# Three pairs of attention-side gate chunks by seven block products

## The chip, the cores and the metric

One core of one Trainium2 chip runs the whole program. The metric is device time in microseconds (us). The engines are TensorE (PE, with its weight loads listed as PEld), VectorE (DVE), ScalarE (ACT), GpSimd (POOL) and SyncE (SP); each works through a queue of its own in order. DMAs are issued from SP's, ACT's and POOL's queues.

## The reference

One decoder block on 512 tokens of 1024 features, in fp32: a feed-forward layer, a token-mixing layer, a second feed-forward layer. What matters here is the mixing layer on its normalised input `u`:

```
z = u @ w_in
gate_br, x_br, q, k, v, g_lru, g_attn = jnp.split(z, IN_SPLITS, axis=-1)
...
y_lru = rg_lru(conv(x_br)) * gelu(gate_br)
y_attn = sliding_window_attention_with_sinks(rope(q), rope(k), v, attn_sinks)
merged = sigmoid(g_lru) * (y_lru @ w_proj_lru) + sigmoid(g_attn) * (y_attn @ w_proj_attn)
return merged @ w_out
```

The change concerns `g_attn = u @ w_in[:, 4608:]`, a product of 512 x 1024 with 1024 x 1024.

## The kernel before

**Split products.** Every fp32 operand is split into a high part (a cast to fp32r) and a low part (the rest). `mm3` (L166 to L169) issues three matmuls for one product: high x high, high x low, low x high. For weights, `wload` starts a DMA on SP's queue into a `wraw` buffer (L105), `wround` casts it on ACT (L115), `wsplit` subtracts on DVE (L123); `wget` returns the next split weight and asks for the two behind it. The order of weights is the list `worder` (L70 to L91).

**Chunks.** Features lie on partitions, tokens along the free dimension. `feat_chunk` (L238) computes 128 output features for all 512 tokens: 8 blocks of 128 inputs, three matmuls of 512 columns each, 24 in all. Normalised features are `u2`, four buffers: high and low parts of two halves, written by `to_features` at the end of the first feed-forward layer.

**The mixing layer** (L1122 to L1214) goes on in this order: `x_group(0)`, keys (`k_pair`), values, `x_group(1)`, two `q_pair`s, eight `gate_chunk`s (`gt`) with attention steps between, two more `q_pair`s, and then eight times `sig_gate` for the LRU side (`glg` the gate chunk, `glp` the projection chunk) and eight times for the attention side (`gag`, `gap`). `k_pair` and `q_pair` rotate on POOL, write to DRAM and load back in another layout (`qt<-q_halves`). `attend(g, n)` handles head group g and token block n; the list `todo` gives their order; its first matmuls are named `at<g><n>b`. `tick` advances work that was begun with `start`.

**The attention side** (L1199 to L1214): `sig_gate(c, ya, "ga")` computes gate chunk c, its tanh on ACT (`gas`), projection chunk c from the split attention output `ya0`, `ya1`; then two DVE instructions (L1201, L1202) multiply and add the LRU side's `m1` into `mg`. POOL starts the DMAs that form sums of blocks of the output weight (`osums`). `oop_split` (L1183) splits what the output projection `token_out` needs (`oy`).

**Seven products.** The feed-forward layers already compute some of their columns by `paired` (L346): the 2 x 2 blocks of two chunks' weights (loaded as `L` and `R`) are summed on DVE (`M`, `N`, L365), split into `W1` to `W4` (L375, L376), and multiplied with sums of blocks of the features that `moving` (L738) makes and splits, and `blocks` takes straight from the features. Seven products of 12 matmuls of 256 columns then give two chunks, accumulated in three PSUM banks X, Y and Q, with copies of X in between (`sn`, `sw`) and adds on DVE.

**Order and buffers.** Where no `manual_schedule` stands, a planner puts the instructions in order before the program runs: among those that its own model of durations counts as ready it takes the earliest in program order. `token_out` and the second feed-forward layer stand in the order written. SBUF buffers of 8 KB per partition (`b8`) come from a pool of 19, those of 4 KB (`t4`) from a pool of 8, those of 2 KB (`t2`) from 10; PSUM has 8 banks. A buffer's next user waits until all users of the previous tile are done.

Of the kernel before, what the change touches and what calls it, by code (L numbers as in the profile page):

```python
# [8 lines left out]
F32 = mybir.dt.float32  # L9
F32R = mybir.dt.float32r  # L10
AF = mybir.ActivationFunctionType
ALU = mybir.AluOpType
# [4 lines left out]
P = 128  # L17
# [6 lines left out]
T = 512  # L24
NT = T // P
# [14 lines left out]

@with_exitstack
def hybrid_block_kernel(ctx, tc, x, xt, g1, w_first, gains, gu1, gs1, dn1, w_x, w_gate, w_q, w_k, w_v, w_gl, w_ga, w_pl, w_pa,
                        w_o, gu2, gs2, dn2, vecs, bd, sinks, rope, mask, out):
    nc = tc.nc
    V, A, G, PE, SP = nc.vector, nc.scalar, nc.gpsimd, nc.tensor, nc.sync

# [17 lines left out]
    def b8(name, shape, dtype=F32):  # L64
        return big.tile(shape, dtype, name=name, tag="b8")
# [9 lines left out]
    for gu, dn in ((gu1, dn1), (gu2, dn2)):  # L75
        worder += [gu[j, i] for j in range(gu.shape[0]) for i in range(2)]
        caps.append(len(worder))
        sums = [dram.tile([P, KS * 512], F32, name=f"wsum{len(wsum)}{i}") for i in range(4)]
        s1, s2, s3, s4 = sums
        wsum[len(wsum)] = (dn, sums)  # L80
        for w in (dn[0], dn[1], s4, s2, s1, s3, dn[3]):
            worder += [w[:, i:min(i + 1024, KS * 512)] for i in range(0, KS * 512, 1024)]
        if gu is gu1:
            worder += [w_x[c] for c in range(4)] + [w_k[i] for i in range(2)] + [w_v[i] for i in range(2)]
            worder += [w_x[c] for c in range(4, 8)] + [w_q[i] for i in range(4)]
            worder += [w_gate[c] for c in range(8)] + [w_q[i] for i in range(4, 8)]
            worder += [w[c] for c in range(8) for w in (w_gl, w_pl)]
            worder += [w[c] for c in range(8) for w in (w_ga, w_pa)]
            t1, t2_, t3, t4_ = osum
            for w in (w_o[0], w_o[1], t2_, t1, w_o[3], t3, t4_):  # L90
                worder += [w[:, i:i + 1024] for i in (0, 1024)]  # L91
# [861 lines left out]
    def x_group(gi):  # L953
        a4, m4, bx4 = (b8(f"{n}{gi}", [P, 4, T]) for n in ("la", "lm", "lb"))
        hl.append(m4)
        cr = range(4 * gi, 4 * gi + 4)
        if gi == 0:
            high_half(u2, x_low, lambda c, b: start(lru_chunk(c, b, a4, m4, bx4, c == cr[-1])),
                      key_weights, 1)
        else:  # L960
            for c in cr:
                w = wget()
                b = bank(f"x{c}")
                feat_chunk(b, w, u2, ALL)
                tick()
                start(lru_chunk(c, b, a4, m4, bx4, c == cr[-1]))
# [139 lines left out]
    def sig_gate(c, src, name):  # L1106
        w = wget()
        b = bank(f"{name}g{c}")
        feat_chunk(b, w, u2, ALL)
        s = t2(f"{name}s{c}")  # L1110
        A.activation(s, b, AF.Tanh, scale=0.5)
        tick()
        wh, wl = wget()
        b = bank(f"{name}p{c}")
        for k in range(KD):
            ks = slice(k * P, (k + 1) * P)
            sh, sl = src[k // 4]
            mm3(b, wh[:, ks], wl[:, ks], sh[:, k % 4, :], sl[:, k % 4, :], k == 0, k == KD - 1)
        tick()
        return s, b  # L1120

    qts = {}  # L1122
    norms = []
    x_group(0)
    kp = [b8(f"kp{i}", [P, 2, 2, T], F32R) for i in range(2)]
    vt = b8("vt", [P, NT, NKV, 2, HD], F32R)
    start(k_pair(kp))
# [2 lines left out]
    for m in range(2):  # L1130
        start(q_pair(m))
    y0 = b8("ya0", [P, 4, T])
    todo = [(g, n) for n in range(NT) for g in range(2)]

    def next_attend(*a):
        if todo:
# [34 lines left out]
    start(split_y(y1, "ya1"))  # L1171
    while live:
        tick()
    mg = [b8(f"mg{i}", [P, 4, T]) for i in range(2)]
    lo_, hi_ = slice(0, 256), slice(256, 512)
    a11, a21, a12, a22 = (mg[i][:, :, tok] for i in range(2) for tok in (lo_, hi_))
    oop = {}
# [18 lines left out]
        V.tensor_tensor(out=o, in0=a, in1=b, op=f)  # L1196
        return o

    for c in range(KD):  # L1199
        s, b = sig_gate(c, ya, "ga")  # L1200
        V.scalar_tensor_tensor(out=s, in0=s, scalar=1.0, in1=b, op0=ALU.add, op1=ALU.mult)  # L1201
        V.tensor_tensor(out=mg[c // 4][:, c % 4, :], in0=s, in1=m1[c // 4][:, c % 4, :], op=ALU.add)  # L1202
        if c < 4:
            o, a, _ = oplan[c]
            with tc.issue_after(norms[-1].ins):
                G.dma_start(osum[o], w_o[a])
        if c in (1, 2, 3, 5):
            o, _, b = oplan[min(c, 4) - 1]
            G.dma_start(osum[o], osum[o // 2] if b is None else w_o[b], accum_op=ALU.add)
        if c == 4:  # L1210
            oop_split(1, a11)
        if c == 5:
            oop_split(7, osum_tile("os3", a11, a21, ALU.subtract))
            oop_split(2, a12, ks=slice(0, 2))  # L1214

    g_post, g_pre = gain_pair(3, 2, "g_b2")
    hs2 = [dram.tile([P, D], F32, name=f"h2_spill{t}") for t in range(NT)]
# [123 lines left out]
def _layout(inputs):  # L1341
    import numpy as np

    c = np.ascontiguousarray
    f = {k: np.asarray(v)[0] for k, v in inputs.items()}
    a = {}
    a["x"] = c(f["x"])
    a["xt"] = c(f["x"].T.reshape(KD, P, T))
    a["g1"] = c(f["ffn1_pre_g"].reshape(KD, P).T)
    a["w_first"] = None  # L1350
    a["gains"] = np.stack([f[n] for n in ("ffn1_pre_g", "ffn1_post_g", "mix_pre_g", "mix_post_g",
                                          "ffn2_pre_g", "ffn2_post_g")])

    def gu(w):
        return c(w.reshape(KD, P, 2, KF, P).transpose(3, 2, 1, 0, 4).reshape(KF, 2, P, D))

    def chunks(w):
        return c(w.reshape(KD, P, KD, P).transpose(2, 1, 0, 3).reshape(KD, P, D))

    a["w_first"] = c(f["ffn1_w_gu"].reshape(KD, P, 2, KF, P)[:, :, :, :2].transpose(0, 1, 3, 2, 4).reshape(KD, P, 512))  # L1360
    def pairs_of(w, j):
        b = w.reshape(2, 4, P, 2, KF // 2, 2, P).transpose(4, 3, 5, 0, 2, 1, 6)[j // 2:].reshape(-1, 2, 2, P, 512)
        return c(np.stack([np.concatenate([b[:, 0, 1], b[:, 0, 0]], 2), np.concatenate([b[:, 1, 0], b[:, 1, 1]], 2)], 1))

    a["gu1"], a["gs1"] = gu(f["ffn1_w_gu"])[2:JSTD["f1"]], pairs_of(f["ffn1_w_gu"], JSTD["f1"])
    ks = [np.concatenate([np.arange(*(GROUPS[g][0], sum(GROUPS[g]))) for g in h]) for h in KHALVES]

    def down_blocks(w):
        w = w.reshape(KF, P, 2, 512)
        return c(np.stack([w[ks[j], :, i].transpose(1, 0, 2).reshape(P, KS * 512) for i in range(2) for j in range(2)]))  # L1370

    a["dn1"] = down_blocks(f["ffn1_w_down"])
    w = f["w_in"]
    a["w_x"], a["w_gate"] = chunks(w[:, D:2 * D]), chunks(w[:, :D])
    half = HD // 2

    def pairs(w):
        return w.reshape(D, -1, 4, 2, half).transpose(0, 1, 3, 2, 4).reshape(D, -1)

    def chunks_of(w):  # L1380
        n = w.shape[1] // P
        return c(w.reshape(KD, P, n, P).transpose(2, 1, 0, 3).reshape(n, P, D))

    a["w_q"], a["w_k"] = chunks_of(pairs(w[:, 2048:3072])), chunks_of(pairs(w[:, 3072:3328]))
    a["w_v"] = c(w[:, 3328:3584].reshape(2, 4, P, 256).transpose(0, 2, 1, 3).reshape(2, P, 1024))
    a["w_gl"], a["w_ga"] = chunks(w[:, 3584:4608]), chunks(w[:, 4608:])
    a["w_pl"] = chunks(f["w_proj_lru"])
    wa = f["w_proj_attn"].reshape(2, 2, 4, HD, D).transpose(0, 2, 1, 3, 4).reshape(D, D)
    a["w_pa"] = chunks(wa)
    w = f["w_out"].reshape(2, 4, P, 2, 512)  # L1390
    a["w_o"] = c(np.stack([w[j, :, :, i].transpose(1, 0, 2).reshape(P, 2048) for i in range(2) for j in range(2)]))
    a["gu2"], a["gs2"] = gu(f["ffn2_w_gu"])[:JSTD["f2"]], pairs_of(f["ffn2_w_gu"], JSTD["f2"])
    a["dn2"] = down_blocks(f["ffn2_w_down"])
    vec = [f["conv_w"][i] for i in range(4)] + [f[n] for n in _VECS]
    a["vecs"] = c(np.stack(vec).reshape(8, KD, P).transpose(2, 0, 1))
    bd = np.zeros((2, 2, HD, KD, 2, HD), np.float32)
    wb = np.stack([f["lru_w_a"], f["lru_w_x"]]).reshape(2, KD, 2, HD, HD)
    for r in range(2):
        bd[:, r, :, :, r, :] = wb[:, :, r].transpose(0, 2, 1, 3)
    a["bd"] = bd.reshape(2, P, D)  # L1400
    a["sinks"] = f["attn_sinks"]
    inv = (10000.0 ** (-np.arange(half) / half)).astype(np.float32)
    ang = np.arange(T, dtype=np.float32)[:, None] * inv[None, :]
    cs = np.stack([np.cos(ang), np.sin(ang)]).astype(np.float32).transpose(2, 0, 1)
    a["rope"] = c(np.tile(cs, (4, 1, 1)))
    qi, si = np.arange(P)[:, None], np.arange(2 * P)[None, :]
    a["mask"] = np.where((si > qi) & (si <= qi + P), 0.0, -1e30).astype(np.float32)
    return a
# [24 lines left out]
```

## Time and profile before

| | |
|---|---|
| median of 3 runs | 1106.77 us (1106.17 to 1107.04) |
| profiled execution | 1106.74 us, of which the span of instructions is 1105.0 us |
| PE busy | 1095.5 us, 6582 matmuls |
| DVE busy | 901.6 us |
| ACT busy | 602.9 us |
| POOL busy | 88.0 us |
| DMA | 213.60 MB, 193 GB/s on average |

A view of lines gives for each instruction its start, its length, the engine, the line of the kernel (that of a helper where one issues it), the operation, the tiles written and read, the shape, and in brackets how long the engine had been idle and what ended that. A group view gives minimum, median and maximum in ns. Rows of DMA issues give the size of one and the median time from issue to landing. The windows view gives a stretch of time: its length, the busy time and number of instructions of PE, PEld, DVE, ACT and POOL, then the granted clock, the share of the DMA engines and GB/s.

### The profile page before, as it was taken

To read this page: it belongs to the slowest core of one execution; us is meant where nothing else is said; L and a number is where in the kernel's file an instruction comes from. 1 tells how busy PE (TensorE), PEld (TensorE's weight loads), DVE (VectorE), ACT (ScalarE), POOL (GpSimd) and SP (SyncE) were. 2 spreads that over 40 slices of the span, in tenths; PEclk is the share of its full clock that TensorE was granted. 3 is DMA by queue.
4 is the path that set the end of the run, shared out by engine and by line. 5 is a ranking of instruction groups with operands and counts; after the bars stand their busy time and mean duration, and the time that the engine had idled before them with its cause. 6 is when DMAs were issued, how large, how long until landed. Compare 5 with 4: busy or idle time off the path is not lost.

```text
span 1105.0 us, 16932 instructions
## 1 busy us (share of the span) xinstructions
PE 1095.5 (99%) x6582; PEld 980.4 (89%) x6582; DVE 901.6 (82%) x1357; ACT 602.9 (55%) x1003; POOL 88.0 (8%) x90
## 2 busy tenths in 40 slices
PE   9999999999999999999999999999999999999997
PEld 7889999988889888788888888888999999998886
DVE  6998988888898788988767461579789888988896
ACT  7435545465756758576555442257545455556662
POOL 1000010000001001123112200001000000000001
PEclk9999999999999999999999999999999999999999
DMA  9238999674687272712822791446439999455483
GB/s 364 78 128 248 305 298 290 202 248 124 190 278 260 92 210 97 190 50 66 265 79 85 263 282 56 133 149 242 144 107 291 314 277 307 116 169 188 150 273 126
DMA packets 55295, 213.60 MB, mean 193 GB/s; under 512 B 6576, under 2 KB 6704, under 8 KB 49456
## 3 DMA queue, kind: packets, MB, share of 16 engines
q1 hardware_dynamic: 46288, 166.92, 44.5%
q0 software_dynamic: 4608, 31.46, 13.6%
q10 hardware_dynamic: 4320, 14.16, 3.5%
q8 instruction: 51, 0.84, 0.3%
q14 instruction: 28, 0.23, 0.1%
HBM read 200.98 MB, written 66.06 MB: 242 GB/s over the span
## 4 chain that ended last, share of the span: by engine, by line
PE 94%; DVE 3%; DMA 1%; issue 1%; ACT 1%; SPq 0%; DVEq 0%; POOLq 0%; POOL 0%; ACTq 0%
PE f1X L169 5%; PE f1X L167 4%; PE f1X L168 4%; PE f2X L169 4%; PE f2X L167 4%; PE f2X L168 4%; PE f2Q L167 2%; PE f2Q L169 2%; PE f2Q L168 2%; PE f1Q L167 2%; PE f1Q L169 2%; PE f1Q L168 2%; PE f1f L834 2%; PE glg L167 1%; PE f1g L167 1%; PE glp L167 1%
## 5 line engine op out<-in xcount | busy, mean ns | idle before, releaser
L123 DVE TENSOR_TENSOR w<-wraw,w 128x1024 fp32r<-128x1024 f32 x174 | 204.1, 1192 | 24.8 <-ACT w L115 24.4
L115 ACT CAST w<-wraw 128x1024 fp32r<-128x1024 f32 x174 | 169.4, 1013 | 32.2 <-PE glp L169 8.3
L169 PE MATMUL f1X<-u1m,f1W 128*128 128x256 f32 x256 | 72.6, 283 | 0.1
L168 PE MATMUL f1X<-u1m,f1W 128*128 128x256 f32 x256 | 72.4, 283 | 0.0
L167 PE MATMUL f1X<-u1m,f1W 128*128 128x256 f32 x256 | 72.4, 283 | 0.0
L169 PEld LDWEIGHTS f1X<-u1m,f1W 128*128 128x128 f32 x256 | 49.1, 192 | 0.3 <-DVE f1W L376 0.3
L167 PEld LDWEIGHTS f1X<-u1m,f1W 128*128 128x128 f32 x256 | 49.1, 192 | 0.1
L168 PEld LDWEIGHTS f1X<-u1m,f1W 128*128 128x128 f32 x256 | 49.1, 192 | 0.1
L1201 DVE SCALAR_TENSOR_TENSOR gas<-gas,gap 128x512 f32<-128x512 f32 x8 | 5.5, 687 | 45.3 <-PE gap L169 45.3
L169 PE MATMUL f2X<-u3m,f2W 128*128 128x256 f32 x144 | 40.9, 284 | 0.1
L169 PE MATMUL f2X<-u3h,f2W 128*128 128x256 f32 x144 | 40.8, 283 | 0.0
L167 PE MATMUL f2Q<-u3m,f2W 128*128 128x256 f32 x144 | 40.8, 283 | 0.0
L168 PE MATMUL f2Q<-u3m,f2W 128*128 128x256 f32 x144 | 40.8, 283 | 0.0
L169 PE MATMUL f2Q<-u3m,f2W 128*128 128x256 f32 x144 | 40.8, 283 | 0.0
L167 PE MATMUL f2X<-u3m,f2W 128*128 128x256 f32 x144 | 40.8, 283 | 0.0
L168 PE MATMUL f2X<-u3l,f2W 128*128 128x256 f32 x144 | 40.8, 283 | 0.0
L168 PE MATMUL f2X<-u3m,f2W 128*128 128x256 f32 x144 | 40.7, 283 | 0.0
L167 PE MATMUL f2X<-u3h,f2W 128*128 128x256 f32 x144 | 40.7, 283 | 0.0
L168 PE MATMUL f1Q<-u1m,f1W 128*128 128x256 f32 x128 | 36.2, 283 | 0.0
L169 PE MATMUL f1Q<-u1m,f1W 128*128 128x256 f32 x128 | 36.2, 283 | 0.0
L167 PE MATMUL f1Q<-u1m,f1W 128*128 128x256 f32 x128 | 36.2, 283 | 0.0
L167 PE MATMUL f1X<-w,f1y 128*128 128x512 f32 x88 | 34.4, 391 | 0.0
(880 smaller groups left out, 3793.1 us busy)
## 6 DMA issues: line engine op xcount, KB each, us to landing
wraw<-wsum SPq DMA_DIRECT2D x40, 512.0 KB, 3.9
wsum<-in_dn_dram SPq DMA_DIRECT2D x16, 1024.0 KB, 10.5
wraw<-in_dn_dram SPq DMA_DIRECT2D x30, 512.0 KB, 5.0
f2L<-in_gs_dram SPq DMA_DIRECT2D x18, 512.0 KB, 5.4
f2R<-in_gs_dram SPq DMA_DIRECT2D x18, 512.0 KB, 5.1
wraw<-in_gu_dram SPq DMA_DIRECT2D x16, 512.0 KB, 7.0
f1L<-in_gs_dram SPq DMA_DIRECT2D x16, 512.0 KB, 5.7
f1R<-in_gs_dram SPq DMA_DIRECT2D x16, 512.0 KB, 5.7
```

The source lines that it names most:

```text
L115: A.copy(w[:, 0, :], raws[n])
L123: V.tensor_tensor(out=w[:, 1, :], in0=raws[n], in1=w[:, 0, :].bitcast(F32), op=ALU.subtract)
L167: PE.matmul(o, lhsT=ah, rhs=bh, start=start, stop=False, skip_group_check=reopen)
L168: PE.matmul(o, lhsT=ah, rhs=bl, start=False, stop=False, skip_group_check=reopen)
L169: PE.matmul(o, lhsT=al, rhs=bh, start=False, stop=stop, skip_group_check=reopen)
L834: PE.matmul(bs[i], lhsT=lw[:, i * P:(i + 1) * P], rhs=rx, start=k == 0 and n == 0, stop=k == KD - 1 and n == 2)
L1201: V.scalar_tensor_tensor(out=s, in0=s, scalar=1.0, in1=b, op0=ALU.add, op1=ALU.mult)
```

## The change

Gate chunks 0 and 1 of the attention side stay as they are. Chunks 2 to 7 become three pairs, (2, 3), (4, 5), (6, 7), each by seven block products, with halves of the projection chunks between the products: pair k runs around projection chunks 2k + 1 and 2k + 2, and the last projection chunk follows alone. The weights of the pairs come as `gsa`, laid out on the host in the blocks that `L` and `R` hold, six loads of 512 KB in place of the six gate chunks' loads of the same size.

`moving` needs `u2` unsplit. Right after `x_group(0)`, POOL's queue writes the two high halves to DRAM (1 MB each) and then adds the two low halves with accumulating DMAs; SP's queue loads the sum (`rawa`, twice 1 MB) at the start of the attention side, where `moving` turns it into the operands of products 4 to 7. Products 1 to 3 read blocks of `u2` directly.

The merged features are accumulated in the buffers of `m1`, without two new ones. `oop_split` for the output projection moves from between the chunks to behind the last pair. In `todo`, head group 0's token blocks 0 and 1 now come before group 1's.

```diff
@@ worder @@
-            worder += [w[c] for c in range(8) for w in (w_ga, w_pa)]
+            worder += [w[c] for c in range(2) for w in (w_ga, w_pa)] + [w_pa[c] for c in range(2, 8)]
@@ after x_group(0) @@
+    u2d = dram.tile([P, 4, 4 * T], F32, name="u2_raw")
+    for i in range(2):
+        G.dma_start(u2d[:, i, :], u2[0][i].rearrange("p k t -> p (k t)").bitcast(F32))
+    for i in range(2):
+        G.dma_start(u2d[:, i, :], u2[1][i].rearrange("p k t -> p (k t)").bitcast(F32), accum_op=ALU.add)
@@ attention order @@
-    todo = [(g, n) for n in range(NT) for g in range(2)]
+    todo = [(0, 0), (0, 1), (1, 0), (1, 1)] + [(g, n) for n in range(2, NT) for g in range(2)]
@@ attention side @@
-    mg = [b8(f"mg{i}", [P, 4, T]) for i in range(2)]
+    mg = m1
...
-    for c in range(KD):
-        s, b = sig_gate(c, ya, "ga")
...
+    def ga_chunk(c):          # gate chunk c, tanh into S[c], tick()
...
+    def pa_chunk(c):          # projection chunk c, a yield after its first half, then gated(c, b)
...
+    def ga_load(k): ...       # L and R of pair k from gsa, on SP
+    def ga_sums(k): ...       # four sums on DVE
+    def ga_parts(k, w): ...   # cast on ACT, subtraction on DVE
+    def ga_product(i, k, begin): ...
+
+    def ga_pair(k, c1, c2):
+        d = gst[k]
+        p1, p2 = pa_chunk(c1), pa_chunk(c2)
+        d["X"], d["Y"], d["Q"] = (bank(f"ga{z}{k}") for z in "XYQ")
+        X, Y, Q = (d[z][:, lo_] for z in "XYQ")
+        sn, sw, a, b = (t2(f"ga{z}{k}") for z in ("sn", "sw", "a", "b"))
+        ga_product(1, k, True)
+        ga_product(2, k, True)
+        A.copy(sn[:, lo_], X)
+        V.tensor_tensor(out=a[:, lo_], in0=Y, in1=sn[:, lo_], op=ALU.add)
+        next(p1)
+        ga_parts(k, 3)
+        ga_product(6, k, False)
+        ga_product(7, k, True)
+        A.copy(sn[:, hi_], X)
+        next(p1)
+        ga_parts(k, 4)
+        ga_load(k + 1)
+        ga_product(5, k, False)
+        A.copy(sw[:, lo_], X)
+        V.tensor_tensor(out=b[:, hi_], in0=Q, in1=sw[:, lo_], op=ALU.add)
+        next(p2)
+        ga_product(3, k, False)
+        A.activation(a[:, hi_], X, AF.Tanh, scale=0.5)
+        ga_product(4, k, False)
+        V.tensor_tensor(out=b[:, lo_], in0=Q, in1=sn[:, hi_], op=ALU.add)
+        A.activation(a[:, lo_], a[:, lo_], AF.Tanh, scale=0.5)
+        A.activation(b, b, AF.Tanh, scale=-0.5)
+        S[2 * k + 2], S[2 * k + 3] = a, b
+        if k + 1 < npair:
+            ga_sums(k + 1)
+            ga_parts(k + 1, 1)
+        next(p2)
+        if k + 1 < npair:
+            ga_parts(k + 1, 2)
+
+    mva = {}
+    rawa = [b8(f"u2r{i}", [P, 4, T]) for i in range(2)]
+    for i in range(2):
+        SP.dma_start(rawa[i].rearrange("p k t -> p (k t)"), u2d[:, i, :])
+    ga_load(0)
+    start(moving(rawa, "u2", mva))
+    ga_chunk(0)
+    run([pa_chunk(0)])
+    tick()
+    ga_chunk(1)
+    while live:
+        tick()
+    blocks(u2, mva)
+    ga_sums(0)
+    ga_parts(0, 1)
+    ga_parts(0, 2)
+    for k in range(npair):
+        ga_pair(k, 2 * k + 1, 2 * k + 2)
+    oop_split(1, a11)
+    oop_split(7, osum_tile("os3", a11, a21, ALU.subtract))
+    oop_split(2, a12, ks=slice(0, 2))
+    run([pa_chunk(KD - 1)])
```

More of the change, by code (lines that the diff above doesn't have):

```diff
@@ L42, in hybrid_block_kernel @@
 def hybrid_block_kernel(ctx, tc, x, xt, g1, w_first, gains, gu1, gs1, dn1, w_x, w_gate, w_q, w_k, w_v, w_gl, w_ga, w_pl, w_pa,
-                        w_o, gu2, gs2, dn2, vecs, bd, sinks, rope, mask, out):
+                        gsa, w_o, gu2, gs2, dn2, vecs, bd, sinks, rope, mask, out):
     nc = tc.nc
@@ L1197, in osum_tile, with gated @@
         return o
-    for c in range(KD):
-        s, b = sig_gate(c, ya, "ga")
-        V.scalar_tensor_tensor(out=s, in0=s, scalar=1.0, in1=b, op0=ALU.add, op1=ALU.mult)
-        V.tensor_tensor(out=mg[c // 4][:, c % 4, :], in0=s, in1=m1[c // 4][:, c % 4, :], op=ALU.add)
+    S = {}
+    def gated(c, b):
+        V.scalar_tensor_tensor(out=S[c], in0=S[c], scalar=1.0, in1=b, op0=ALU.add, op1=ALU.mult)
+        z = mg[c // 4][:, c % 4, :]
+        V.tensor_tensor(out=z, in0=S[c], in1=z, op=ALU.add)
         if c < 4:
@@ L1207, in hybrid_block_kernel @@
         if c in (1, 2, 3, 5):
[L1208 to L1214, printed above, removed]
+            o, _, a = oplan[min(c, 4) - 1]
+            G.dma_start(osum[o], osum[o // 2] if a is None else w_o[a], accum_op=ALU.add)
+    def ga_chunk(c):
+        w = wget()
+        b = bank(f"gag{c}")
+        feat_chunk(b, w, u2, ALL)
+        S[c] = t2(f"gas{c}")
+        A.activation(S[c], b, AF.Tanh, scale=0.5)
+        tick()
@@ new lines, in pa_chunk, with ga_load @@
+    def pa_chunk(c):
+        wh, wl = wget()
+        b = bank(f"gap{c}")
+        for k in range(KD):
+            ks = slice(k * P, (k + 1) * P)
+            sh, sl = ya[k // 4]
+            mm3(b, wh[:, ks], wl[:, ks], sh[:, k % 4, :], sl[:, k % 4, :], k == 0, k == KD - 1)
+            if k == 3:
+                yield
+        gated(c, b)
+        yield
+    npair = gsa.shape[0]
+    gst = [{} for _ in range(npair)]
+    def ga_load(k):
+        if k < npair:
+            for i, z in ((1, "L"), (0, "R")):
+                gst[k][z] = t4(f"ga{z}{k}").rearrange("p (a b) -> p a b", a=2)
+                SP.dma_start(gst[k][z].rearrange("p a b -> p (a b)"), gsa[k, i])
@@ new lines, in ga_sums, with ga_parts @@
+    def ga_sums(k):
+        d = gst[k]
+        L, R = d["L"], d["R"]
+        d["M"] = M = t4(f"gaM{k}").rearrange("p (a b) -> p a b", a=2)
+        d["N"] = N = t2(f"gaN{k}")
+        for o, a, b in ((M[:, 1], R[:, 1], L[:, 0]), (L[:, 0], L[:, 0], L[:, 1]), (M[:, 0], R[:, 1], L[:, 0]),
+                        (N, R[:, 0], M[:, 0])):
+            V.tensor_tensor(out=o, in0=a, in1=b, op=ALU.add)
+    def ga_parts(k, w):
+        d = gst[k]
+        raw = d["RMLN"[w - 1]]
+        if w == 4:
+            t = t4(f"gaW4{k}", F32R).rearrange("p (s b) -> p s b", s=2)
+        else:
+            t = b8(f"gaW{w}{k}", [P, 2, 2, 512], F32R)
+        A.copy(t[:, 0], raw)
+        V.tensor_tensor(out=t[:, 1], in0=raw, in1=t[:, 0].bitcast(F32), op=ALU.subtract)
+        d[f"W{w}"] = t
@@ new lines, in ga_product @@
+    def ga_product(i, k, begin):
+        d = gst[k]
+        o = d[" XYXQXXQ"[i]][:, lo_]
+        w, slot = {1: (1, 1), 2: (1, 0), 3: (4, None), 4: (3, 1), 5: (3, 0), 6: (2, 0), 7: (2, 1)}[i]
+        t = d[f"W{w}"]
+        wh, wl = (t[:, 0], t[:, 1]) if slot is None else (t[:, 0, slot], t[:, 1, slot])
+        bh, bl = mva[i]
+        for k4 in range(4):
+            ks = slice(k4 * P, (k4 + 1) * P)
+            mm3(o, wh[:, ks], wl[:, ks], bh[:, k4, :], bl[:, k4, :], begin and k4 == 0, k4 == 3, True)
@@ new lines, in ga_pair @@
+    def ga_pair(k, c1, c2):
+        d = gst[k]
+        p1, p2 = pa_chunk(c1), pa_chunk(c2)
[31 more added lines that the diff above has]
+            ga_parts(k + 1, 2)
@@ new lines, in hybrid_block_kernel @@
+    mva = {}
[9 more added lines that the diff above has]
+    while live:
+        tick()
+    blocks(u2, mva)
[6 more added lines that the diff above has]
+    oop_split(7, osum_tile("os3", a11, a21, ALU.subtract))
@@ L1389, in _layout @@
     a["w_pa"] = chunks(wa)
+    b = w[:, 4608:].reshape(2, 4, P, 4, 2, P).transpose(3, 4, 0, 2, 1, 5)[1:].reshape(-1, 2, 2, P, 512)
+    a["gsa"] = c(np.stack([np.concatenate([b[:, 0, 1], b[:, 0, 0]], 2), np.concatenate([b[:, 1, 0], b[:, 1, 1]], 2)], 1))
     w = f["w_out"].reshape(2, 4, P, 2, 512)
```

## The prediction, made before the change was run

> **What bounds the kernel now.** I read the head of the page first, then the chain, then who kept TensorE (PE) waiting.
>
> ```profile
> span 1105.0 us, 16932 instructions
> PE 1095.5 (99%) x6582; PEld 980.4 (89%) x6582; DVE 901.6 (82%) x1357; ACT 602.9 (55%) x1003; POOL 88.0 (8%) x90
> PE 94%; DVE 3%; DMA 1%; issue 1%; ACT 1%; SPq 0%; DVEq 0%; POOLq 0%; POOL 0%; ACTq 0%
> ```
>
> ```profile
> PE at10b L1047 <- DMA qt<-q_halves: 1.5, 1, 1.5
> PE warm L186 <- DVE warm L181: 1.5, 1, 1.5
> ```
>
> PE carries the chain, and in the whole span it has only two waits of over a microsecond: the start, and one in attention. So time is won in two ways, fewer columns through PE, or that attention wait. For the stage that the change rewrites, the windows view gives (length, then busy us of PE, PEld, DVE, ACT, POOL; clock; DMA share; GB/s), and below it the lines of two short stretches:
>
> ```profile
> 637.10:724.14 87.04, 87.04 (x385) 72.10 (x384) 36.69 (x40) 26.46 (x33) 1.61 (x2) 1.00 0.51 151
> 615.00:655.00 40.00, 40.00 (x186) 33.30 (x185) 20.52 (x27) 20.40 (x34) 6.47 (x8) 1.00 0.99 291
> ```
>
> The reader should see that this stage never lets PE stop, that the clock is full (1.00), that DVE is used for 36.69 of 87.04 us and ACT for 26.46, and that DMA is saturated (share 0.99) just as the stage begins.
>
> The duration of one matmul in the rows (0.39, 0.28) is latency; the pace is the distance between starts:
>
> ```profile
> 637.10 0.39 PE L167 MATMUL gag<-u2h,w 128*128 128x512 f32 x1
> 642.54 0.39 PE L167 MATMUL gap<-ya0h,w 128*128 128x512 f32 x1
> 724.14 0.39 PE L167 MATMUL woX<-w,oy 128*128 128x512 f32 x1
> 889.64 0.28 PE L167 MATMUL f2Y<-u3h,f2W 128*128 128x256 f32 x1
> 891.08 0.28 PE L167 MATMUL f2X<-u3m,f2W 128*128 128x256 f32 x1
> ```
>
> From 637.10 to 642.54 stand 24 matmuls of 512 columns: 5.44/24 = 0.2267 us each. The whole stage is 16 such groups: 384 x 0.2267 = 87.04, all of its length. From 889.64 to 891.08 stand the 12 matmuls of 256 columns of one block product: 1.44/12 = 0.120 us. Half the columns cost 53% of the time, which takes back a third of what seven products for eight should give.
>
> **The change part by part.**
>
> *Six gate chunks become three pairs.* Per pair, 48 matmuls x 0.2267 = 10.88 us go and 84 x 0.120 = 10.08 us come: -0.80 us, three times -2.40 us. By the Trainium skill (TensorE: Matmul & The Clock Gate, Back-to-back issue gap) a warm matmul takes N/2.4 + 2.5 ns, so 215.8 and 109.2 ns, and the three pairs would give 3 x (10.36 - 9.17) = -3.57 us; the trace disagrees in both widths (226.7 and 120.0 ns), and I keep the trace's.
>
> *The order of attention.* The gates of group 1, token block 0 (at10) move behind those of group 0, block 1 (at01). The rows around the wait (of the chain, then of PE):
>
> ```profile
> 452.99 4.27 DMA q_halves<-q1st
> 458.59 8.03 DMA qt<-q_halves
> 464.90 0.39 PE L169 MATMUL gt<-u2h,w 128*128 128x512 f32 x1
> 466.75 1.08 PE L1047 MATMUL at10b<-kp,qt 128*128 128x128 f32 x8 [1.47 <-DMA qt<-q_halves]
> 473.39 0.95 PE at01b L1047 x8
> ```
>
> PE stood from 464.90 + 0.23 = 465.13 to about 466.75: 1.62 us, since the second query pair lands at 466.62. at01 reads only the first pair, loaded before, and the wait's owner now comes a gate chunk later (24 x 0.2267 = 5.44 us), behind the landing. Gain 1.62 us; bounds 0 (another late transfer takes the place) and 1.62; I take 1.62, since the margin of about 5 us is three times the wait.
>
> *u2 put together in DRAM.* Two 1 MB writes and two 1 MB accumulating writes on POOL's queue, and later two 1 MB loads on SP's. The features are complete with the last `u2l` (353.30 + 1.29 = 354.6). Nothing in the trace shows such a write from SBUF with add. The nearest rows (KB each, us to landing) and POOL's next instruction:
>
> ```profile
> q_halves<-q0st SPq DMA_DIRECT2D x1, 1024.0 KB, 4.6
> wsum<-wsum POOLq DMA_DIRECT2D x8, 1024.0 KB, 11.1
> osums<-in_w_o_dram POOLq DMA_DIRECT2D x6, 1024.0 KB, 14.4
> 353.30 1.29 DVE L233 TENSOR_TENSOR u2l<-b1ntp,u2h 128x512 fp32r<-128x512 f32 x2 [1.39 <-ACT u2h L233]
> 383.98 1.29 POOL L1002 TENSOR_TENSOR kkm<-kkm,kkm 128x512 f32<-128x512 f32 x1 [36.23 <-ACT tr L922]
> ```
>
> The second pair waits on POOL for the first to land. Behind it on POOL stands the key rotation `kkm`, and on that ACT's and DVE's `kkst`, then the keys. POOL must only get past the wait, 354.6 + 4.6 to 354.6 + 14.4 = 369.0; `kkm` is due at 383.98. Cost 0, with 15 us in hand at the slow end. If the cover were gone, a late `kkm` would hold ACT's queue in a stage where DVE and ACT feed PE closely; bounds 0 to 2 us. The result lands by 369 + 14.4 = 383 and is read at about 637: hidden.
>
> *Preparation on DVE and ACT.* The same steps stand in the last feed-forward block:
>
> ```profile
> L746 ACT ACTIVATE u3m<-u3ts x4: 1042/1058/1061, 786.9 to 795.0; 128x1024 fp32r<-128x1024 f32 x4
> L747 DVE SCALAR_TENSOR_TENSOR u3m<-u3ts,u3m x4: 1220/1224/1225, 788.0 to 796.1; 128x1024 fp32r<-128x1024 f32 x4
> L750 DVE TENSOR_TENSOR u3ts<-u3r x1: 1225/1225/1225, 784.3 to 784.3; 128x1024 f32<-128x1024 f32 x1
> L365 DVE TENSOR_TENSOR f2M<-f2R,f2L x36: 681/689/694, 803.7 to 972.2; 128x512 f32<-128x512 f32 x36
> L376 DVE TENSOR_TENSOR f2W<-f2M,f2W x18: 1211/1212/1220, 807.6 to 975.4; 128x1024 fp32r<-128x1024 f32 x18
> L376 DVE TENSOR_TENSOR f2W<-f2N,f2W x18: 681/682/685, 819.2 to 989.3; 128x512 fp32r<-128x512 f32 x18
> L396 ACT COPY f2sn<-f2X x36: 359/372/377, 813.5 to 986.5; 128x256 f32<-128x256 f32 x36
> L402 DVE TENSOR_TENSOR f2ca<-f2Y,f2sn x18: 415/416/425, 816.6 to 982.1; 128x256 f32<-128x256 f32 x18
> ```
>
> `moving`, once: DVE 8 x 1.22 = 9.8 us, ACT 4 x 1.06 = 4.2. A pair: 4 sums x 0.69 + 3 x 1.21 + 0.68 + 3 adds x 0.42 = 8.3 us of DVE, less two chunk splits (2 x 1.21) that go: +5.9. In all DVE 36.7 + 9.8 + 3 x 5.9 = 64 us in a stage of 84.6: 76%, below the 82% of the whole span. Hidden as a sum. In a pair, the copy of X that product 6 must await (0.37 us, L396) has product 2 (1.44 us) and half a projection chunk (12 x 0.2267 = 2.72 us) over it, and so have the later ones. At the end the last projection chunk (5.44 us) covers the splits for the output projection as before, since pair 2 prepares no successor. Cost 0.
>
> *Loads.* The six gate loads of 512 KB become six of the same size; new are the two 1 MB loads of raw u2, which need two of the 19 big buffers. These come free when the last matmul on the LRU-side features ends (the `glp` row at 635.97, quoted below with the first rival), so at about 636. That is the start of the stage, with DMA at share 0.99. At the 291 GB/s of the window alone, 2 MB take 7.2 us (landed 644); at half of it 14.4 (landed 651). Product 6 of the first pair, the first reader, is due at 637.1 + 3 x 5.44 + 2.88 + 2.72 = 659, and `moving`'s first operand needs 2 x 1.22 + 1.06 + 1.22 = 4.7 us: 656 at the latest. Hidden, if nothing urgent is queued behind it on DVE (first rival). By the Trainium skill (DMA: Bandwidth & Descriptors, Issuing engines are not separate DMA queues) these loads share the 16 engines with POOL's `osums`; that fits the share of 0.99.
>
> **Sum.** Against the profiled execution's 1106.74 us (span 1105.0 plus 1.74 around it; 0.03 under the median 1106.77): -2.40 - 1.62 = 1102.72, plus 0.2 for ripple at new seams: 1102.9 us.
>
> **The rivals.**
>
> *Late raw features block DVE.* `moving` stands ahead of the second gate chunk's weight split in program order. If the planner puts its first subtraction ahead, and the load lands late, DVE stops with that split behind it.
>
> ```profile
> 635.97 0.39 PE L169 MATMUL glp<-ylh,w 128*128 128x512 f32 x1
> 639.29 2.50 DVE L291 TENSOR_TENSOR ya1l<-ya,ya1h 128x512 fp32r<-128x512 f32 x4 [0.69 <-ACT ya1h L290]
> 641.81 2.36 DVE L123 TENSOR_TENSOR w<-wraw,w 128x1024 fp32r<-128x1024 f32 x2
> ```
>
> The split at 641.81 feeds the chunk due on PE at 637.10 + 2 x 5.44 = 647.98. With a landing at 644 the split is done at 644 + 3.5 (a sum, a cast, a split) + 1.2 = 648.7, some 1 us late; at 651, 8 us late; middle 4.5, so 1102.9 + 4.5 = 1107.4. For it: the share of 0.99, and that the planner has already misjudged one transfer, at10's. Against it: at 641.8 the split is ready and the features are probably not yet, in the planner's count too; then it goes first.
>
> *The attention wait only moves.* Then -2.40 alone: 1104.5. For it: the second pair took 4.27 and 8.03 us on its two trips, and may take longer. Against: the 5 us margin.
>
> *The pairs starve for buffers (slower).* Alive in a pair are u2 4, y 4, merged 2, moving operands 4: 14 of 19; three split weight blocks and three projection weights make 20. If each pair's third block gets its buffer only when PE needs it, PE waits one cast and one split, 1.06 + 1.21 = 2.3 us; three pairs 6.8: 1109.7. It decides from one such wait in every pair. For it: 20 against 19. Against: block 1 is finished after 2.88 us of the pair and hands over its buffer two chunks' halves before product 5, and idle PE slots can take projection halves.
>
> *Matmuls at the page's gaps*, not the rows': -3.57 - 1.62, so 1101.6.
>
> **How the numbers follow.** Both gains with small seams (1102.5 to 1103.5): 0.42. Late features: 0.25, of which 0.08 cost under 1.8 us (still faster), 0.12 up to 6 us, 0.05 more. Wait moved: 0.12, on the limit, 0.07 faster. Starved: 0.10, slower. The page's gaps: 0.05. Something small and unseen that eats the gain: 0.06, no change. A difference under 0.2% (2.2 us: 1104.6 to 1109.0) can't be told from none here. Faster 0.42 + 0.08 + 0.07 + 0.05 = 0.62; same 0.12 + 0.05 + 0.06 = 0.23; slower 0.05 + 0.10 = 0.15. The range runs from 1102.2 (no seams, half a microsecond of luck) to 1107.4 (late features at their middle); it leaves out the starved case, the page's gaps and the worst of the late features, 0.2. The likeliest case's own range is 1102.5 to 1103.5.
>
> **What would show it.** Right: 252 matmuls of 256 columns at 0.12 us spacing in place of 144 of 512; no PE wait before `at10b`; none before the second gate chunk; the stage about 84.6 us. Wrong: a DVE wait on the load of raw u2 with an L123 split after it; PE waits on the W blocks; `kkm` later than the rest of its stage.

## The result, and the profile after

| | before | after |
|---|---|---|
| median | 1106.90 us (1106.17 to 1108.62, 4 runs) | 1115.63 us (1115.54 to 1116.17, 4 runs) |
| ratio, 95% interval | | 1.0087 (1.0074 to 1.0099) |
| profiled execution, its span | 1106.74, 1105.0 us | 1115.54, 1113.6 us |

The changed kernel is 8.7 us slower, where 4 us faster was predicted. Three rows of its page, with the granted clock by slices of 1113.6/40 = 27.8 us:

```profile
span 1113.6 us, 17219 instructions
PE 1096.8 (98%) x6690; PEld 985.1 (88%) x6690; DVE 928.0 (83%) x1392; ACT 615.4 (55%) x1025; POOL 93.0 (8%) x94
PEclk9999999999999999999999989999999999999999
```

The rows as such say little: PE still looks 98% busy. But one slice of the clock has dropped to 8, and the list of PE's waits has a new first entry:

```profile
PE gag L167 <- ACT w L115: 8.1, 1, 8.1
PE warm L186 <- DVE warm L181: 1.5, 1, 1.5
PE gaX L167 <- ACT gaW L1263: 0.4, 1, 0.4
PE gag L169 <- DVE w L123: 0.2, 1, 0.2
```

The wait before `at10b` is gone. In its place PE waits once, for 8.1 us, for the cast of a weight on ACT: the weight of the second gate chunk. The rows of lines around it, of SP, DVE, ACT and PE in turn:

```profile
631.86 1.06 SPq L1317 DMA_DIRECT2D u2r<-u_raw  x2
...
644.03 1.23 DVE L750 TENSOR_TENSOR u2ts<-u2r 128x1024 f32<-128x1024 f32 x1 [3.82 <-DMA u2r<-u_raw]
651.39 1.23 DVE L751 TENSOR_TENSOR u2ts<-u2r,u2ts 128x1024 f32<-128x1024 f32 x1 [3.31 <-DMA u2r<-u_raw]
654.88 1.22 DVE L123 TENSOR_TENSOR w<-wraw,w 128x1024 fp32r<-128x1024 f32 x1
...
652.65 1.06 ACT L746 ACTIVATE u2m<-u2ts 128x1024 fp32r<-128x1024 f32 x1 [10.89 <-DVE u2ts L751]
653.61 1.03 ACT L115 CAST w<-wraw 128x1024 fp32r<-128x1024 f32 x1
...
646.17 0.39 PE L169 MATMUL gap<-ya1h,w 128*128 128x512 f32 x1
654.69 0.79 PE L167 MATMUL gag<-u2h,w 128*128 128x512 f32 x1 [8.13 <-ACT w L115]
...
656.15 0.80 PE L169 MATMUL gag<-u2h,w 128*128 128x512 f32 x1 [0.24 <-DVE w L123]
...
657.17 0.63 PE L168 MATMUL gag<-u2l,w 128*128 128x512 f32 x1
657.60 0.63 PE L169 MATMUL gag<-u2h,w 128*128 128x512 f32 x1
...
661.41 0.40 PE L169 MATMUL gag<-u2h,w 128*128 128x512 f32 x1
...
663.46 0.39 PE L169 MATMUL gag<-u2h,w 128*128 128x512 f32 x1
664.24 0.39 PE L167 MATMUL gaX<-u2h,gaW 128*128 128x256 f32 x1 [0.40 <-ACT gaW L1263]
```

Read it from the loads down. The raw features are issued at 631.86 and let DVE go on only at 644.03 and 651.39. ACT's next instruction in its queue is the cast of the first moving operand, which needs both: ACT stands idle for 10.89 us until 652.65, and the cast of the weight, though its data are there, stands behind it until 653.61. (The load of that weight was issued at 602.11, and the slowest landing of a weight from 600 to 660 us took 22.0 us.) PE had finished projection chunk 0 at 646.17 + 0.2267 = 646.40.

Then a second thing. After 654.69 the matmuls of 512 columns start 0.43 us apart (657.17, 657.60) and not 0.2267. The windows view shows why, cut at the moments at which the recorded clock changes and at multiples of 3.413 us around them, to within 0.05 us (length, busy PE, PEld, DVE, ACT, POOL, then the granted clock):

```profile
644.35:647.76 3.41, 2.21 (x10) 1.50 (x8) 1.97 (x3) 0.00 (x0) 0.00 (x0) 1.00 1.01 293
647.76:651.17 3.41, 0.00 (x0) 0.00 (x0) 0.32 (x1) 0.00 (x0) 0.00 (x0) 0.99 1.06 271
651.17:654.59 3.42, 0.00 (x0) 0.00 (x0) 2.08 (x2) 1.94 (x2) 0.00 (x0) 0.50 0.69 213
654.59:658.00 3.41, 3.06 (x6) 2.00 (x7) 3.41 (x4) 0.05 (x1) 0.80 (x1) 0.50 0.45 62
658.00:661.41 3.41, 3.41 (x9) 2.67 (x8) 2.29 (x3) 3.01 (x4) 0.00 (x0) 0.51 0.99 207
661.41:664.83 3.42, 3.02 (x16) 2.28 (x15) 3.42 (x5) 3.27 (x4) 0.00 (x0) 1.00 0.86 271
```

For 10.24 us the clock is at half, and 6.7 us of that lie after PE has its weight again. From 654.69 to 661.41 stand 14 matmuls: 6.72 - 14 x 0.2267 = 3.55 us more than at full speed. Not all of that is the clock. The third of them needs the weight's split, which DVE begins only at 654.88, and starts at 656.15. At full speed PE would have been there at 654.69 + 2 x 0.2267 = 655.14, so 1.01 us would have gone in any case. The other 2.54 us (661.41 - 656.15 - 12 x 0.2267) are the half clock.

The stage, from its first `gag` to the first `woX`:

```profile
635.57:732.92 97.35, 88.58 (x494) 77.02 (x493) 62.50 (x75) 38.84 (x55) 1.61 (x2) 0.95 0.58 166
```

It took 87.04 us before. The predicted 84.64 + 8.30 (wait for the cast) + 1.01 (wait for the split) + 2.54 (half clock) + 0.55 (first block product: 664.24 - 663.46 - 0.2267) + 0.31 (the rest) = 97.35. Elsewhere, from the starts of the first `gt`, `glg` and `gag`: ahead of attention -0.36, attention -1.64 (83.60 to 81.96), LRU side +0.41 (111.11 to 111.52), behind the stage -0.10. Together +8.62, of a span that grew by 8.6.

The parts that went as foreseen are visible too: POOL's writes and the key rotation behind them, and (windows view) attention and three quarters of the pairs' time without an idle moment of PE:

```profile
353.24 1.19 POOL L1127 DMA_DIRECT2D u_raw<-u2h  x2 [5.82 <-ACT u2h L233]
383.56 1.29 POOL L1002 TENSOR_TENSOR kkm<-kkm,kkm 128x512 f32<-128x512 f32 x1 [18.34 <-DVE kkm L1000]
```

```profile
442.08:524.04 81.96, 81.96 (x418) 69.41 (x416) 74.66 (x170) 53.48 (x128) 21.99 (x12) 1.00 0.37 102
671.00:718.00 47.00, 47.00 (x306) 43.03 (x305) 33.46 (x43) 20.66 (x31) 0.00 (x0) 1.00 0.39 120
```

### The profile page after: what moved, and what is told of

Read it like the earlier page. It is cut to its first block, busy times and chain, and to the rows that moved or that the text cites. A ratio compares the mean times of both kernels' runs of the same rounds, so it can differ in the third digit from the quotient of the medians.

```text
span 1113.6 us, 17219 instructions
## 1 busy us (share of the span) xinstructions
PE 1096.8 (98%) x6690; PEld 985.1 (88%) x6690; DVE 928.0 (83%) x1392; ACT 615.4 (55%) x1025; POOL 93.0 (8%) x94
## 4 chain that ended last, share of the span: by engine, by line
PE 85%; DVE 8%; ACT 3%; issue 2%; DMA 2%; DVEq 0%; POOLq 0%; POOL 0%; ACTq 0%; SPq 0%
PE f1X L169 4%; PE f1X L168 4%; PE f1X L167 4%; PE f2X L169 4%; PE f2X L168 4%; PE f2X L167 4%; PE f2Q L169 2%; PE f2Q L168 2%; PE f2Q L167 2%; PE f1Q L169 2%; PE f1Q L168 2%; PE f1Q L167 2%; PE f1f L834 2%; DVE w L123 2%; DMA u2r<-u_raw 2%
## 5 line engine op out<-in xcount | busy, mean ns | idle before, releaser
L123 DVE TENSOR_TENSOR w<-wraw,w 128x1024 fp32r<-128x1024 f32 x168 | 199.3, 1201 | 24.3 <-ACT w L115 24.0
L115 ACT CAST w<-wraw 128x1024 fp32r<-128x1024 f32 x168 | 163.9, 1011 | 27.2 <-PE glp L169 7.4
L167 PE MATMUL f1X<-w,f1y 128*128 128x512 f32 x88 | 34.4, 391 | 0.0
L169 PE MATMUL f1X<-w,f1y 128*128 128x512 f32 x88 | 34.3, 389 | 0.0
```

Of the source, the lines that this page charges most:

```text
L115: A.copy(w[:, 0, :], raws[n])
L123: V.tensor_tensor(out=w[:, 1, :], in0=raws[n], in1=w[:, 0, :].bitcast(F32), op=ALU.subtract)
L167: PE.matmul(o, lhsT=ah, rhs=bh, start=start, stop=False, skip_group_check=reopen)
L169: PE.matmul(o, lhsT=al, rhs=bh, start=False, stop=stop, skip_group_check=reopen)
```

## The experiments

The question was whether the late landing alone costs the time, or the order of casts and splits in ACT's and DVE's queues, which puts the urgent ones behind instructions that wait for the landing. Ratios are to the kernel before on the same chip, with 95% intervals.

**Landing early, order kept.** The first copies of `osums` on POOL, which run beside the loads, are held until the raw features have landed.

```diff
-            with tc.issue_after(norms[-1].ins):
+            with tc.issue_after(landed.ins):
                 G.dma_start(osum[o], w_o[a])
...
+    landed = G.tensor_tensor(out=sm("landed"), in0=rawa[1][:, 0, :1], in1=mhalf, op=ALU.mult)
     ga_load(0)
```

> The changed kernel with one edit: POOL starts the output-weight sums (osums) only after the raw u2 loads have landed; the order of ACT's and DVE's instructions up to the pairs stays as it is. Theory A (the two loads land late because osums share the DMA engines, and ACT's queue holds the second gate chunk's weight cast behind the first moving-operand cast): the loads land within about 7 us of their issue in place of 12 and 19, PE's 8.1 us wait before the second gate chunk goes, the clock stays at 1.00 behind it, and 11.9 us come back: 1115.6 - 11.9 = 1103.7 us. Rival B (the order itself or the buffers are too tight, whatever the load does): a wait of several us stays, 1109 or more. Rival C (the slow clock is a state of its own, not the wait's consequence): the wait goes and the slow matmuls stay, about 1107.

Measured: 1112.39 us, ratio 1.0061 (1.0048 to 1.0074). The loads did land early, from the view of the tile `u2r`, and PE waited all the same:

```profile
DMA to landing us min/median/max: 5.0/6.0/7.0
```

```profile
PE gag L169 <- DVE w L123: 3.4, 1, 3.4
PE gaX L167 <- ACT gaW L1263: 2.9, 2, 1.7
```

The rows of DVE show the reason: it had the raw features at 640.63, but next in its queue stands the multiplication with projection chunk 0, which PE delivers only at 647.17, then a moving operand's split, and only then the split that PE is waiting for.

```profile
641.88 1.23 DVE L751 TENSOR_TENSOR u2ts<-u2r,u2ts 128x1024 f32<-128x1024 f32 x1
647.17 0.69 DVE L1207 SCALAR_TENSOR_TENSOR gas<-gas,gap 128x512 f32<-128x512 f32 x1 [4.06 <-PE gap L169]
...
648.50 1.22 DVE L747 SCALAR_TENSOR_TENSOR u2m<-u2ts,u2m 128x1024 fp32r<-128x1024 f32 x1
649.64 1.22 DVE L123 TENSOR_TENSOR w<-wraw,w 128x1024 fp32r<-128x1024 f32 x1
```

The stage is 93.55 us: landing early gives back 3.8 of the 12.7 us. That the late landing is the whole cause is refuted. The second row of waits is in part a price: with `osums` moved later, the second pair's `R`, issued at 665.50, takes 12.4 us to land, and PE waits 1.7 us at about 677. In the changed kernel the slowest `R` takes 5.5 us.

**Only the next two splits first.** The casts and splits of the second gate chunk and the second projection chunk go ahead of `start(moving(...))`; the first pair's blocks stay behind it.

```diff
     ga_load(0)
+    wsplit(wpos[0] + 4)
     start(moving(rawa, "u2", mva))
```

> The changed kernel with one edit: the next two weights (second gate chunk, second projection chunk) are cast and split ahead of the moving operands; osums run as before the edit, so the raw loads land late again. Theory A with only that one instruction at fault: no wait before the second gate chunk, 1103.7 us. Theory A with the whole ACT queue at fault (the first pair's W1 cast stands behind all four moving-operand casts too): the second gate chunk is on time, and the wait moves to the first block product, due about 652, with W1 ready about 662: 8 to 10 us again, clock drop again, 1113 to 1116. Rival B: as now, 1115.6, with the wait at the same place.

Measured: 1113.11 us, 1.0075 (1.0060 to 1.0089). The second gate chunk comes on time, and the wait has moved to the next instruction that stands behind the moving casts, the first weight block of the first pair:

```profile
PE gaX L167 <- ACT gaW L1263: 8.4, 1, 8.4
```

So it is not one misplaced split: everything on ACT behind the moving casts is late.

**No trip through DRAM.** The unsplit features are summed on DVE from the two parts in place of the writes and loads.

```diff
-    u2d = dram.tile([P, 4, 4 * T], F32, name="u2_raw")
...
-        SP.dma_start(rawa[i].rearrange("p k t -> p (k t)"), u2d[:, i, :])
+        V.tensor_tensor(out=rawa[i], in0=u2[0][i].bitcast(F32), in1=u2[1][i].bitcast(F32), op=ALU.add)
```

> The changed kernel without the way through DRAM: raw u2 is the sum of its high and low halves, made by two DVE additions of 128x2048 at the start of the attention side. Theory A: nothing waits on a DMA there; the additions cost DVE about 2 x 2.4 us from about 640, so the second gate chunk's split is ready about 651 against 646.4: a wait of 4 us or so, a short slow clock or none, 1107 to 1109. Rival B: as long as now, 1115.

Measured: 1110.49 us, 1.0045 (1.0031 to 1.0059); stage 91.95. There is no load to be late, and three waits are left, two at the second gate chunk and one at the first weight block:

```profile
PE gag L167 <- ACT w L115: 2.5, 1, 2.5
...
PE gaX L167 <- ACT gaW L1258: 1.2, 1, 1.2
PE gag L169 <- DVE w L123: 1.0, 1, 1.0
```

Without a load to wait for, the same order costs less, but it still costs, the two sums of 2.28 us on DVE included. This speaks for the order as the cause and the late landing as what sets its price.

**The attention order alone,** in the kernel before.

```diff
-    todo = [(g, n) for n in range(NT) for g in range(2)]
+    todo = [(0, 0), (0, 1), (1, 0), (1, 1)] + [(g, n) for n in range(2, NT) for g in range(2)]
```

> The kernel before with only the new order of attention (group 0's blocks 0 and 1 ahead of group 1's). If the wait for the second query pair is simply jumped: no wait before at10b, 1106.8 - 1.6 = 1105.2 us. If the transfer is late whatever comes first: the wait stays near its 1.5 us, 1106.8.

Measured: 1105.40 against 1105.52 us, 0.9998 (0.9988 to 1.0007). The wait is gone and attention is 81.96 us long, as predicted; but the LRU side is 112.12 us, 1.0 more than before, with a new small wait there:

```profile
PE at20b L1047 <- DVE at13pl L1072: 0.4, 1, 0.4
```

**Urgent work first, loads as they are.** The splits of the second gate chunk and the second projection chunk and the first weight block go ahead of `moving`, the sums and the second block ahead of the tick that runs the moving operands' later half.

```diff
     ga_load(0)
+    wsplit(wpos[0] + 4)
+    ga_parts(0, 1)
     start(moving(rawa, "u2", mva))
     ga_chunk(0)
     run([pa_chunk(0)])
+    ga_sums(0)
+    ga_parts(0, 2)
     tick()
...
     blocks(u2, mva)
-    ga_sums(0)
-    ga_parts(0, 1)
-    ga_parts(0, 2)
```

> The changed kernel with only the order of preparation edited: the splits of the second gate chunk and second projection chunk and the first pair's W1 stand ahead of the moving operands, and the sums with W2 ahead of the last two moving operands; osums and the raw loads stay as they were, so the loads land 12 and 19 us after their issue again. Theory D (a late load costs only what is queued behind it on ACT and DVE): both waits of the runs so far (second gate chunk, first block product) go, the first moving operand is ready about 655 against 657, the clock stays at 1.00, and the time is that of before less 2.4 and 1.2 to 1.6 us: ratio 0.9965 to 0.998 with up to 2 us of small waits. Rival B (buffers): the waits move on to W2 or W3 of the first pair, several us, ratio over 1.003.

Measured: 1106.28 us, 1.0007 (0.9998 to 1.0016). The loads are as late as in the changed kernel (tile view), yet the waits are small (PE's waits):

```profile
DMA to landing us min/median/max: 12.5/15.9/19.4
```

```profile
PE gaQ L169 <- DVE gaW L1264: 0.8, 1, 0.8
PE gaQ L167 <- ACT gaW L1263: 0.5, 1, 0.5
```

The rows of ACT show why. It stands before the first moving operand as long as in the changed kernel (10.42 us, there 10.89), but the casts that are due are done ahead of it:

```profile
639.64 2.00 ACT L115 CAST w<-wraw 128x1024 fp32r<-128x1024 f32 x2
...
653.51 2.26 ACT L746 ACTIVATE u2m<-u2ts 128x1024 fp32r<-128x1024 f32 x2 [10.42 <-DVE u2ts L751]
```

```profile
636.07:723.35 87.28, 85.86 (x494) 75.18 (x493) 62.09 (x75) 38.42 (x55) 1.61 (x2) 1.00 0.60 175
```

The stage is 87.28 us and the clock stays full: 10.07 of the 12.71 us are back by order alone. This is the run that tells the two theories apart. What remains, 2.64 us over 84.64, is slightly more than the pairs' gain of 2.40; the predicted 2 to 4 us under the kernel before did not come.

**Both,** the order above and `osums` held back.

```diff
-            with tc.issue_after(norms[-1].ins):
+            with tc.issue_after(landed.ins):
...
+    wsplit(wpos[0] + 4)
+    ga_parts(0, 1)
...
```

> The same order of preparation, and osums started only after the raw loads have landed. Theory D: no better than the run before it at the first gate chunks (nothing urgent waits there any more), and the second pair's weight block R lands late again as in the run with late osums (issued 665, landed 678), which costs PE 2 us: ratio 0.998 to 1.000. If the late load itself is what costs: clearly better than the run before it.

Measured: 1106.96 us, 1.0010 (1.0002 to 1.0019), stage 88.21. The loads land in 4.9 and 6.9 us; PE now waits for the second pair's late `R`:

```profile
PE gaX L167 <- ACT gaW L1263: 2.4, 1, 2.4
```

`R` took 15.3 us to land here, with `osums` beside it, and at most 4.5 us in the version before it. So holding the copies back in this stretch delayed the next thing loaded.

**Order, and no DRAM trip.**

```diff
...
+    ga_load(0)
+    wsplit(wpos[0] + 4)
+    ga_parts(0, 1)
     rawa = [b8(f"u2r{i}", [P, 4, T]) for i in range(2)]
     for i in range(2):
-        SP.dma_start(rawa[i].rearrange("p k t -> p (k t)"), u2d[:, i, :])
+        V.tensor_tensor(out=rawa[i], in0=u2[0][i].bitcast(F32), in1=u2[1][i].bitcast(F32), op=ALU.add)
-    ga_load(0)
     start(moving(rawa, "u2", mva))
...
+    ga_sums(0)
+    ga_parts(0, 2)
...
```

> The same order of preparation, with raw u2 summed on DVE (4.6 us) in place of the way through DRAM. Theory D: the urgent splits come after the two additions in DVE's queue at the worst, at about 646 against 646.4 due: ratio 0.997 to 0.999. If DVE's load decides: worse than the run with the loads.

Measured: 1104.11 against 1105.73 us, 0.9985 (0.9976 to 0.9994): faster than both kernels, 1.6 us under the one before. PE's waits list nothing but `warm`, and the stage is 85.82 us, 1.18 us over 84.64. Of that, 1.03 us are small gaps between the starts of matmuls, at the first pair's product 7 and right behind it (660.43 to 663.34):

```profile
635.69:721.51 85.82, 85.60 (x494) 75.24 (x493) 65.98 (x77) 38.44 (x55) 1.61 (x2) 1.00 0.57 155
```

**The changed kernel again,** unedited, on the chip of the last three.

> The changed kernel once more beside the same runs of the kernel before. All theories: ratio 1.0087 or so, and the half-speed stretch after the 8 us wait again, its length a multiple of about 3.4 us as in the clock records so far (10.2 us after the 8.3 us wait, 6.8 after one of 8.5, 3.4 after one of 3.6, none after one of 1.6).

Measured: 1115.83 us, 1.0092 (1.0078 to 1.0105). The wait is 8.6 us there, and the half clock lasts 10.24 us again.

**The sums earlier still.** On top of the best version, the sums and the second block directly behind `start(moving(...))`.

```diff
     start(moving(rawa, "u2", mva))
-    ga_chunk(0)
-    run([pa_chunk(0)])
     ga_sums(0)
     ga_parts(0, 2)
+    ga_chunk(0)
+    run([pa_chunk(0)])
     tick()
```

> The version without DRAM and with urgent splits first, with one more move: the first pair's sums and W2 ahead of the second moving operand, too. If W2's late split is all that is left of the waits (1.2 us in the stage): 1.0 us less than that version, ratio to before 0.9975 or so. If the second moving operand then comes late instead (it now stands behind the second projection chunk's addition on DVE): a wait of 2 to 5 us at product 7, ratio 1.000 to 1.004.

Measured: 1107.21 against 1106.01 us, 1.0010 (1.0001 to 1.0019), stage 87.74: 1.9 us worse than without this edit. Now a projection chunk's weight split is the one that stands too far back:

```profile
PE gap L169 <- DVE w L123: 2.0, 1, 2.0
```

**The best version with the old attention order.**

```diff
-    todo = [(0, 0), (0, 1), (1, 0), (1, 1)] + [(g, n) for n in range(2, NT) for g in range(2)]
+    todo = [(g, n) for n in range(NT) for g in range(2)]
```

> The version without DRAM and with urgent splits first, with the old order of attention. If the order is worth what the trace of the kernel before showed: a wait of about 1.6 us before at10b and 1.6 us more than the version with the new order. If, as the new order alone did nothing to the kernel before, that wait is not there in most runs: no difference (within 0.6 us).

Measured: 1105.06 against 1106.01 us, 0.9988 (0.9980 to 0.9997); the new order had 0.9985 (0.9976 to 0.9994). No difference can be told. In the traces the old order has 82.75 + 111.11 = 193.86 us for attention and LRU side, the new one 81.96 + 111.48 = 193.44.

**The kernel before again,** unedited, for a second trace of the same wait.

> The kernel before, unchanged, for a second trace of it. If the wait before at10b belongs to the kernel: 1.5 us there again and 83.6 us from the first gate chunk of the LRU branch to the LRU side's first. If it belongs to one run: about 82.0 us, and that is why the new order alone measured nothing.

Measured: 1106.51 us, with

```profile
PE at10b L1047 <- DMA qt<-q_halves: 1.3, 1, 1.3
```

and 83.36 + 111.11 us for the two stages. So two traces of this kernel have the wait. That the timed runs have it at this length is not shown: this execution took 0.5 us more than the median on its chip (1106.01), and the best version with the old order has it at

```profile
PE at10b L1047 <- DMA qt<-q_halves: 0.3, 1, 0.3
```

## Why the prediction was wrong, step by step

- **Three pairs, -2.40: right.** In the version with no wait listed the stage is 85.82 us, and without the 1.03 us of small gaps 84.79; 84.64 were predicted. The paces taken from the rows held (0.2267 and 0.120 us). One remark in it was off: the slower pace of 256 columns takes back 0.56 of 1.36 us per pair, two fifths and not a third of the gain; the sum did not use it.
- **Attention order, -1.62: right in its stage, partly lost in the next.** Attention became 1.64 us shorter, but the LRU side longer: 0.41 us in the changed kernel, 1.0 us with the order alone. The timed runs show no gain; whether the wait is as long in them as in the traces stays open. The prediction asked what is late next only for the waits at the start of attention.
- **u2 through DRAM on POOL, 0: right.** `kkm` started at 383.56, predicted cover up to 383.98.
- **Preparation, 0: the sum right, the conclusion not.** DVE has 62.50 us of work in the stage, 64 were predicted. That it fits as a sum says nothing of the first 15 us, in which instructions that wait stand in front of those that are due.
- **Loads, "Hidden, if nothing urgent is queued behind it on DVE": the step that failed.** The sum put this term at 0; it cost 12.40 us (8.30 for the cast, 1.01 for the split, 2.54 of half clock, 0.55 for the first weight block). The condition was written down and then answered with "in the planner's count too; then it goes first". The planner put the moving cast first, and on ACT, a queue that the prediction did not name. The slow end of its estimate, landed at 651, came true (651.39), but by luck: the loads started at 631.86 and not at 636, and took 12.1 and 18.8 us, longer than estimated, so two errors cancelled.
- **The rival "late raw features", 0.25: the right mechanism, too small.** It got a quarter of the chance, a middle of 4.5 us, and even at its worst, 8 us, priced the wait only. The wait was 9.31 us up to the split. On top came the half clock and the first weight block, which stands behind all four moving casts.
- **Starved buffers, 0.10: not seen.** After the first block product at 664.24 no wait of PE is listed in the changed kernel, though 20 buffers were wanted where there are 19. **The attention wait moves, 0.12:** no later transfer took its place; with the order alone a small wait of 0.4 us, for DVE and on the LRU side, did, and the rest of the longer LRU side is not explained. **Matmuls at the page's gaps, 0.05:** not seen; the paces are those of the rows.

What stays open: why the planner put the moving cast ahead of a weight's cast whose data were there. It goes by its own durations, in which the loads would have landed in time; that is an inference, since only the order was varied, not the planner's durations.

## What to carry to other kernels

When a change starts a load in a stretch where DMA is saturated, do not ask only whether its own reader can wait: write down, for each engine's queue, what stands behind the first instruction that reads it, and when the bound engine is due there. Put the casts and splits that are due first ahead of that instruction, or make the operand from what is already on the chip; here the second and the first together were needed to keep 1.6 us of a predicted 4. And price a long wait of TensorE with the stretch of half clock that can follow it, 2.54 us here.

## What the runs showed of the hardware

**The clock falls by windows, not by the length of a gap.** Wherever the granted clock fell in this stage, it stayed at half for 3.413, 6.827 or 10.24 us: one, two or three times 3.413. Cut into windows of that length, counted from the moments of change, each fall follows a window in which PE did little or nothing (0.00 in the changed kernel). The last window before a fall, in the changed kernel without the trip through DRAM and in the one with `osums` held back:

```profile
646.86:650.27 3.41, 0.73 (x2) 0.30 (x2) 3.38 (x5) 1.73 (x2) 0.81 (x1) 0.99 0.39 79
```

```profile
648.93:652.34 3.41, 1.43 (x6) 1.22 (x7) 3.41 (x4) 0.00 (x0) 0.82 (x1) 0.99 1.02 356
```

And three windows after which it did not fall: of the second of these kernels later on, of the one with both edits, and of the kernel before at its attention wait:

```profile
676.23:679.65 3.42, 1.74 (x15) 1.54 (x14) 1.60 (x3) 1.32 (x2) 0.00 (x0) 1.00 1.08 365
```

```profile
674.26:677.67 3.41, 1.90 (x10) 1.69 (x11) 2.87 (x4) 1.33 (x2) 0.00 (x0) 1.00 1.10 344
```

```profile
464.15:467.56 3.41, 1.94 (x14) 1.43 (x12) 3.36 (x10) 2.56 (x10) 0.00 (x0) 1.00 0.94 250
```

By these windows the line lies between 1.43 and 1.74 us of busy time in 3.41. The ends of the programs, where PE stops, narrow it: the clock held after a window with 1.58 us in the best version with the old order (1094.22 to 1097.63), and fell after one with 1.11 us in the version with `osums` held back (1102.85 to 1106.26). So it is the work in a window that decides here and not the longest wait alone: a wait of 2.4 us (both edits) cost no fall, one of 2.5 us with another of 1.0 us close behind it (no trip through DRAM) did. One window with some work does not bring the clock back either: it stayed at half after the one with 3.06 us in the changed kernel, and rose after the one with 3.36 us in the kernel without the trip through DRAM (650.27 to 653.69). The Trainium skill (TensorE: Matmul & The Clock Gate, What's actually happening) tells of a free-running window of 3413 ns, half the clock after an idle one, and full speed after a busy one; the length agrees to the nanosecond. The rule of thumb of the Trainium skill (TensorE: Matmul & The Clock Gate, HAM oscillation — how this bites in real kernels) is no idle gap over about 3.4 us. Here the measurement differs: without the trip through DRAM the longest wait was 2.5 us, and the clock fell.

**Two loads beside six copies.** The same two loads of 1 MB took 12.1 and 18.8 us beside POOL's `osums`, and 5.0 and 7.0 us with these held back. The prediction's two estimates, 7.2 and 14.4 us, were both below the second load.
